# A two-layer hybrid backbone: the first stage in a fixed order, latent rows ahead of context rows

## The chip, the core and the metric

The kernel runs on one core of a Trainium2 chip. The metric is device time in microseconds of one execution. Three runs of the kernel before gave a median of 1833.99 us (1833.54 to 1836.31).

## What is computed

Layer 0 gives each row of `x` (256 latent tokens) and of `ctx` (256 context tokens), both 1024 wide, a modulated norm, and projects the result with one matrix. The part of the reference that the first stage computes:

```python
def modulate(x, g, shift, scale):
    return rms_norm(x, g) * (1 + scale) + shift

def ada_params(cvec, w, b):
    mod = jax.nn.silu(cvec) @ w + b
    return jnp.split(mod[..., None, :], 6, axis=-1)

# even_layer
mx = ada_params(c, ada_w, ada_b)          # for the latent rows
mc = ada_params(c_ctx, ada_w, ada_b)      # for the context rows
... = even_project(modulate(ctx, n1_g, mc[0], mc[1]), w_in, qn_g, kn_g)
... = even_project(modulate(x, n1_g, mx[0], mx[1]), w_in, qn_g, kn_g)
```

After it come retention and grouped attention over both streams, an out-projection and a dense SwiGLU (layer 0), then latent attention and top-2-of-8 SwiGLU experts (layer 1). The experts take more than half of the time and are not touched.

## The kernel before

All matmuls are in float32r, with the operand split in two: a rounded copy H (ScalarE, line 104) and the rest L (VectorE, line 105), so that one product takes three matmuls: H·H, L·H and H·L. Matmuls are in `mm` (line 85), transposes in `transpose` (line 213).

The first stage makes, for the 512 rows (token tiles t = 0, 1 latent, 2, 3 context; stream s = 0 latent, 1 context), the modulated input `X` and the product of it with columns 2048 to 2560 of `w_in` (called bq). The 1024 columns of `X` come in eight k tiles, in four parts q of two k tiles each:

- `norm_rows` (lines 303 to 322) takes the mean square of two row tiles on ScalarE (line 314), the reciprocal root by a dozen small VectorE operations (lines 185 to 197), and scales the rows (line 321 on VectorE, line 319 on ScalarE). `xn_T(s)` (line 453) transposes the rows on TensorE, and ScalarE copies them out of PSUM (line 459).
- `ada_loads(q)` (line 419) asks SP's queue for two 1 MB blocks of `l0_ada_w`. `ada_part(q)` (line 425) is 64 small matmuls with them (line 429), an add on VectorE (line 432), one transpose, and two VectorE operations for shift and scale (lines 437, 439).
- `bq_load(k)` (line 470) loads 256 KB of `w_in`. `bq_split(k)` splits it, applies scale and shift to both streams of one k tile (line 482, result `hf`), and splits that into `X`. `bq_mm(k)` (line 489) has 12 matmuls of 512 columns, over all four t.

The loop is at lines 496 to 512: in turn q it asks for the loads of q and the modulation loads of q+1, traces `ada_part(q)`, the matmuls of part q-1, and then the splits of part q. The order on an engine isn't this order: a scheduler with its own model of costs orders the instructions of each engine, by program order where several are ready in its model. `tc.keep_in_program_order(ins)` binds one instruction behind the one traced before it on its engine. Buffers with one tag are reused in turn, and the scheduler adds the waits for that.

The next unit of work, `rows_unit(X, w_in, 2560, ...)` at line 542 (called bkv: 96 matmuls of 256 columns), needs a 1 MB load, its split, and the two PSUM banks of tag mm, which ScalarE frees at line 526. Ahead of it on SP's queue stand, at lines 520 and 521, the rotary table and the broadcast of two 64-wide gains to 128 partitions and 8 and 2 heads; behind it the decay bands (line 543) and other small broadcasts (line 219). `Ada` (line 237) is the same modulation for later rows; it has its bias loads on ScalarE's queue (line 245). The decay masks of retention (`ret_masks`, line 729) take the tile `wb` from `bands`, in two ScalarE operations (lines 736 and 741).

Of the kernel before, what the change touches and what calls it, by code (L numbers as in the profile page):

```python
# [58 lines left out]
@with_exitstack  # L59
def hybrid_kernel(ctx: ExitStack, tc: tile.TileContext, i, out):  # L60
    nc = tc.nc
    ACT, DVE, PE = nc.scalar, nc.vector, nc.tensor


    const = ctx.enter_context(tc.tile_pool(name="const", bufs=1))
# [149 lines left out]
    def bcast_into(t, reps):  # L215

        c = 0
        for s, r, m in reps:
            nc.sync.dma_start(v3(t[:, c:c + r * m], r),
                              bass.AP(tensor=s.tensor, offset=s.offset, ap=[[0, P], [0, r], [1, m]]))  # L220
            c += r * m

# [134 lines left out]
    nc.gpsimd.memset(sil, 0.0)  # L357

    ACT.activation(sil[:, 0, 31:32], sil[:, 0, 30:31], AF.Silu)
    x_r = load_res("rx", i["x"])  # L360

    vec_list = [("c", 8), ("c_ctx", 8), ("l0_norm1_g", 8), ("l0_norm2_g", 8), ("l1_norm1_g", 8), ("l1_norm2_g", 8),
                ("l1_q_lora_g", 3), ("l1_kv_lora_g", 2)]
# [7 lines left out]
    def load_vecs(names):  # L371
        n = sum(dict(vec_list)[v] for v in names)
        vrow = modp.tile([P, 512], F32, tag="adarow", bufs=2, name=nm("vrow"))[:n, :P]
        r = 0
        for v in names:
            src = i[v]
            if len(src.shape) == 2:
                src = src.rearrange("o n -> (o n)")
            m = dict(vec_list)[v]
            (nc.scalar if len(names) > 2 else nc.sync).dma_start(vrow[r:r + m, :], src.rearrange("(a b) -> a b", b=P))  # L380
            r += m
        return vrow, vpos[names[0]], n

    def vecs_T(vrow, c0, n):
        ps = psum("T")
        transpose(ps[:, :n], vrow)
        DVE.tensor_copy(vecT[:, c0:c0 + n], ps[:, :n])

    vec_c = load_vecs(["c", "c_ctx"])
    c_r = load_res("rc", i["ctx"])  # L390

    vecs_T(*vec_c)
    for s, name in enumerate(("c", "c_ctx")):
# [6 lines left out]
    la = l0.enter_context(tc.tile_pool(name="la", bufs=1))  # L400
# [4 lines left out]
    def x_tiles(n):  # L405
        return [xp.tile([P, 4, 512], F32R, tag=tg, name="x1" + tg) for tg in X_TAGS[n]]
# [36 lines left out]
    sh1 = const.tile([P, KD, 2], F32, tag="sh1_0", name="sh1_0")  # L443
    xnT = [xp.tile([P, 4, 512], F32, tag=tg, name="xnT" + tg) for tg in ("a1", "a3")]
    loads = [ada_loads(0)]
    vec_g = load_vecs([n for n, _ in vec_list[2:]])
    for s in range(2):
        for a in range(2):
            nc.scalar.dma_start(adab[64 * a + s:64 * a + 64:32, :, :],
                              b_ada[1024 * a:1024 * a + 1024].rearrange("(q h c) -> h q c", h=2, c=P))  # L450
    xns = [norm_rows(x_r, la, "bv"), norm_rows(c_r, la, "bv", act=(1,))]

    def xn_T(s):
        for kp in range(KD // 2):
            ps = psum("S" if kp % 2 else "T")
            for kk in range(2):
                for t in range(2):
                    transpose(ps[:, kk * 256 + t * P:kk * 256 + (t + 1) * P], xns[s][t][:, tok(2 * kp + kk)])
            ACT.copy(xnT[kp // 2][:, 2 * (kp % 2):2 * (kp % 2) + 2, 256 * s:256 * s + 256], v3(ps[:, :], 2))

    xn_T(0)
    vecs_T(*vec_g)

    TOK = range(4)

# [4 lines left out]
    def bq_load(k):  # L470
        if k % 4 == 0:
            wbq["H", k // 4], wbq["L", k // 4] = ring_tile("H"), ring_tile("L")
        wbq[k] = lt.tile([P, 512], F32, tag="prob", bufs=4, name=nm("wbq"))
        nc.sync.dma_start(wbq[k], w_in[k * P:(k + 1) * P, 2048:2560])

    def bq_split(k):
        c = tok4(k)
        split_to(wbq["H", k // 4][:, c], wbq["L", k // 4][:, c], wbq[k])
        hf = lt.tile([P, 512], F32, tag="hf", bufs=2, name=nm("hf"))
        for s in range(2):  # L480
            cs = slice(256 * s, 256 * s + 256)
            DVE.tensor_scalar(hf[:, cs], xnT[k // 4][:, k % 4, cs], s1[:, k, s:s + 1], sh1[:, k, s:s + 1],
                              op0=ALU.mult, op1=ALU.add)
        split_to(X.H(k, slice(0, 512)), X.L(k, slice(0, 512)), hf)

    def tok4(k):
        return slice(512 * (k % 4), 512 * (k % 4) + 512)

    def bq_mm(k):
        H, L, c = wbq["H", k // 4], wbq["L", k // 4], tok4(k)  # L490
        for t in TOK:
            mm(ps_bq[t], X.H(k, tok(t)), H[:, c], k == 0, False)
            mm(ps_bq[t], X.L(k, tok(t)), H[:, c], False, False)
            mm(ps_bq[t], X.H(k, tok(t)), L[:, c], False, k == KD - 1)

    for q in range(5):
        if q < 4:
            for k in (2 * q, 2 * q + 1):
                bq_load(k)
            if q < 3:  # L500
                loads.append(ada_loads(q + 1))
            if q == 1:
                for l, t in zip((X.hs, X.ls), x_tiles(1)):
                    l.append(t)
            ada_part(q, loads[q])
        if q == 0:
            xn_T(1)
        for k in (2 * q - 2, 2 * q - 1) if q else ():
            bq_mm(k)
        if q < 4:  # L510
            for k in (2 * q, 2 * q + 1):
                bq_split(k)
# [4 lines left out]
    band = v3(cb[:, 0:1152], 3)  # L517
    ropeb = cb[:, 1152:1408].rearrange("p (t w c) -> p t w c", t=2, w=2)
    g10 = cb[:, 1408:2048]
    nc.sync.dma_start(ropeb, i["rope_b"])  # L520
    bcast_into(g10, [(i["l0_q_norm_g"], 8, 64), (i["l0_k_norm_g"], 2, 64)])

    qk = {}
    for t in TOK:
# [15 lines left out]
        DVE.reduce_sum(ss[:, 10 * t:10 * t + 10], v3(sq[:, :], 10), axis=AX.X)  # L540

    rows_unit(X, w_in, 2560, (2, 3, 0, 1), bkv_evac)
    nc.sync.dma_start(band, i["bands"])
    lgt = bcast_row(i["l0_ret_log_decay"].rearrange("a b -> (a b)"), 16, "lgt")
    lg256 = small.tile([P, 16], F32, tag="lg256", bufs=1, name="lg256")
    DVE.tensor_scalar(lg256, lgt, 256.0, None, op0=ALU.mult)
# [182 lines left out]
    def ret_masks(hp):  # L729

        W = []
        for hf in range(2):
            h = 2 * hp + hf
            wf = lt.tile([P, 2, 384], F32, tag="s3", bufs=4, name=nm("wf"))
            wb = lt.tile([P, 2, 384], F32, tag="wb", bufs=1, name=nm("wb"))
            ACT.activation(wb[:, 0, :], band[:, 2, :], AF.Identity, scale=lgt[:, 8 + h:9 + h])
# [1096 lines left out]
```

## Time and profile before

| | |
|---|---|
| median of three runs | 1833.99 us |
| the profiled execution | 1834.48 us |
| its span | 1832.7 us |
| TensorE busy | 1788.2 us, 98% of the span |
| VectorE, ScalarE, GpSimd busy | 1391.4, 1119.9, 14.2 us |
| from the start to the first bkv matmul | 58.10 us |

The time outside the span is 1.8 us. A row of the timeline has the start, the busy time of the merged instructions, engine, line, operation, output and inputs, and how many; in brackets stand the idle time ahead of it on its engine and what ended that. A row of the chain has start, duration and what it was. A row of the windows has busy time and instruction count of each engine, the granted clock of TensorE (1.00 is full speed), the busy share of the 16 DMA engines, and GB/s. A busy TensorE is not TensorE at its peak, since the ends of matmuls are modelled: rates are taken from starts.

### The profile page before, as it was taken

What the parts mean: (1) busy time and instruction counts of PE and PEld (TensorE: products, weight loads), DVE (VectorE), ACT (ScalarE), POOL (GpSimd) and SP (SyncE); (2) the same over time, 40 slices, a digit from 0 to 9 for tenths busy, and PEclk for the clock granted to TensorE, in tenths of its full rate; (3) what the DMA queues carried; (4) which work ended last, traced back from release to release, by engine and by line L of the source; (5) the groups of instructions that cost most, each with busy time, mean ns of one, the idle gap of its engine ahead of it and who ended that gap; (6) DMA issues with size and microseconds to landing.
All of it is one profiled execution on the core that took longest, in us unless ns stands there. A gap on an engine that the chain in (4) does not pass through costs nothing.

```text
span 1832.7 us, 23905 instructions
## 1 busy us (share of the span) xinstructions
PE 1788.2 (98%) x9410; PEld 1461.5 (80%) x9410; DVE 1391.4 (76%) x1739; ACT 1119.9 (61%) x1191; POOL 14.2 (1%) x24
## 2 busy tenths in 40 slices
PE   7899999999999999999999999999999999999997
PEld 5778668878779998677888888878878888788786
DVE  4688676424345668788889889898898898888887
ACT  4686543421223464567877777777767777777775
POOL 0000000000000000020000000000000000000000
PEclk9999999999999999999999999999999999999999
DMA  8443542343344566868998999999999999999992
GB/s 284 161 138 120 179 117 92 95 155 110 126 148 152 174 199 204 335 216 310 349 367 320 371 363 360 374 335 350 368 342 379 371 341 344 358 362 374 348 376 79
DMA packets 228730, 483.36 MB, mean 264 GB/s; under 512 B 11013, under 2 KB 65626, under 8 KB 223490
## 3 DMA queue, kind: packets, MB, share of 16 engines
q1 hardware_dynamic: 228416, 481.64, 73.7%
q8 instruction: 76, 1.25, 0.3%
q14 instruction: 44, 0.36, 0.1%
q10 hardware_dynamic: 194, 0.12, 0.0%
HBM read 480.68 MB, written 1.05 MB: 263 GB/s over the span
## 4 chain that ended last, share of the span: by engine, by line
PE 86%; DVE 6%; DMA 3%; ACT 2%; issue 1%; ACTq 0%; SPq 0%; DVEq 0%
PE ps L85 80%; PE ps L213 3%; DVE uL L105 3%; PE ps L258 2%; DMA uraw<-in_l_w_in_dram 1%; ACT uH L104 1%; DMA uraw<-in_l_exp_w_dram 0%; DMA uraw<-in_l_w_out_dram 0%; DMA raw<-in_l_exp_w_dram 0%; DVE rx L1705 0%; DMA rx<-in_x_dram 0%; PE ps L429 0%; DVE y L105 0%; DVE rst L194 0%; DMA xn<-in_l_exp_w_dram 0%
## 5 line engine op out<-in xcount | busy, mean ns | idle before, releaser
L85 PE MATMUL ps<-uH,xe 128*128 128x512 f32 x1792 | 450.8, 391 | 4.4 <-ACT uH L104 3.2
L85 PEld LDWEIGHTS ps<-uH,xe 128*128 128x128 f32 x1792 | 334.0, 188 | 76.2 <-ACT uH L104 5.3
L105 DVE TENSOR_TENSOR uL<-uraw,uH 128x2048 fp32r<-128x2048 f32 (+3 forms) x126 | 276.2, 2193 | 136.8 <-ACT uH L104 128.8
L104 ACT CAST uH<-uraw 128x2048 fp32r<-128x2048 f32 (+3 forms) x126 | 231.1, 1835 | 203.4 <-PE ps L85 163.5
L85 PE MATMUL ps<-uL,xe 128*128 128x512 f32 x896 | 244.4, 392 | 2.7 <-DVE uL L105 2.3
L105 DVE TENSOR_TENSOR uL<-h,uH 128x2048 fp32r<-128x2048 f32 x95 | 217.2, 2290 | 24.6 <-ACT uH L104 20.6
L85 PE MATMUL ps<-uH,aa 128*128 128x512 f32 x896 | 222.4, 390 | 0.0
L104 ACT CAST uH<-h 128x2048 fp32r<-128x2048 f32 x95 | 181.8, 1916 | 54.4 <-PE ps L85 47.9
L85 PEld LDWEIGHTS ps<-uL,xe 128*128 128x128 f32 x896 | 166.0, 188 | 41.9 <-DVE uL L105 8.6
L85 PEld LDWEIGHTS ps<-uH,aa 128*128 128x128 f32 x896 | 168.0, 188 | 35.2 <-issue 0.5
L85 PE MATMUL ps<-h,uH 128*128 128x256 f32 (+1 forms) x1008 | 176.7, 327 | 0.0
L85 PEld LDWEIGHTS ps<-h,uH 128*128 128x128 f32 x1008 | 150.8, 190 | 21.9 <-issue 3.2
L105 DVE TENSOR_TENSOR uL<-a,uH 128x2048 fp32r<-128x2048 f32 x60 | 137.4, 2290 | 16.8 <-ACT uH L104 14.6
L105 DVE TENSOR_TENSOR uL<-raw,uH 128x2048 fp32r<-128x2048 f32 (+1 forms) x60 | 135.2, 2254 | 15.2 <-ACT uH L104 14.2
L104 ACT CAST uH<-raw 128x2048 fp32r<-128x2048 f32 (+1 forms) x60 | 113.2, 1887 | 35.9 <-PE ps L85 35.4
L104 ACT CAST uH<-a 128x2048 fp32r<-128x2048 f32 x60 | 114.9, 1915 | 33.0 <-PE ps L85 32.9
L85 PE MATMUL ps<-uL,aa 128*128 128x512 f32 x448 | 123.4, 396 | 0.0
L85 PEld LDWEIGHTS ps<-uL,aa 128*128 128x128 f32 x448 | 81.4, 188 | 15.6 <-DVE uL L105 0.5
L85 PE MATMUL ps<-h,uL 128*128 128x256 f32 (+1 forms) x504 | 92.6, 326 | 0.0
L85 PE MATMUL ps<-uH,a 128*128 128x512 f32 x352 | 88.2, 391 | 1.1 <-ACT uH L104 1.1
L105 DVE TENSOR_TENSOR uL<-xp,uH 128x2048 fp32r<-128x2048 f32 (+1 forms) x34 | 76.9, 2262 | 10.3 <-ACT uH L104 9.9
L85 PEld LDWEIGHTS ps<-h,uL 128*128 128x128 f32 x504 | 76.9, 190 | 7.8
(384 smaller groups left out, 2364.4 us busy)
## 6 DMA issues: line engine op xcount, KB each, us to landing
h<-in_l_exp_w_dram SPq DMA_DIRECT2D x94, 1024.0 KB
uraw<-in_l_exp_w_dram SPq DMA_DIRECT2D x60, 1024.0 KB
a<-in_l_exp_w_dram SPq DMA_DIRECT2D x60, 1024.0 KB
raw<-in_l_exp_w_dram SPq DMA_DIRECT2D x58, 1024.0 KB
uraw<-in_l_ffn_w_dram SPq DMA_DIRECT2D x38, 1024.0 KB
uraw<-in_l_ada_w_dram SPq DMA_DIRECT2D x34, 1024.0 KB
xp<-in_l_exp_w_dram SPq DMA_DIRECT2D x30, 1024.0 KB
xn<-in_l_exp_w_dram SPq DMA_DIRECT2D x30, 1024.0 KB
```

What stands on the lines that cost most here:

```text
L85: PE.matmul(o, l, r, start=start, stop=stop)
L104: h = ACT.copy(H, src)
L105: l = DVE.tensor_sub(L, src, H.bitcast(F32))
L213: PE.transpose(o, in_, ident[:in_.shape[0], :in_.shape[0]])
L258: PE.matmul(self.ps[32 * j:32 * j + 32, :], sil[:, self.k, :], raw[:, 512 * j:512 * j + 512], start=(self.k == 0), stop=(self.k == KD - 1) ...
```

## The change

The diff, with repeated lines cut:

```diff
+    engines = nc.scalar, nc.vector, nc.tensor
+    ACT, DVE, PE = engines
+    class InOrder:
+        def __getattr__(self, name):
+            f = getattr(self.engine, name)
+            return lambda *a, **k: tc.keep_in_program_order(f(*a, **k))
 # bcast_into
-            nc.sync.dma_start(v3(t[:, c:c + r * m], r),
+            nc.gpsimd.dma_start(v3(t[:, c:c + r * m], r),
 # load_vecs
-            (nc.scalar if len(names) > 2 else nc.sync).dma_start(vrow[r:r + m, :], ...)
+            (nc.gpsimd if names[0] != "c" else nc.sync).dma_start(vrow[r:r + m, :], ...)
-    x_r = load_res("rx", i["x"])
     vec_c = load_vecs(["c", "c_ctx"])
-    c_r = load_res("rc", i["ctx"])
+    x_r = load_res("rx", i["x"])
     loads = [ada_loads(0)]
-    vec_g = load_vecs([n for n, _ in vec_list[2:]])
+    vec_g = load_vecs(["l0_norm1_g"])
-            nc.scalar.dma_start(adab[64 * a + s:64 * a + 64:32, :, :],
+            nc.gpsimd.dma_start(adab[64 * a + s:64 * a + 64:32, :, :],
-    xns = [norm_rows(x_r, la, "bv"), norm_rows(c_r, la, "bv", act=(1,))]
+    ACT, DVE, PE = (InOrder(e) for e in engines)
+    xns = [norm_rows(x_r, la, "bv")]
-    xn_T(0)
     vecs_T(*vec_g)
+    xn_T(0, (0, 1))
+    def bq_xsplit(q, s, between=None):
+        for kk in range(2):
+            DVE.tensor_scalar(hf[:, kk, :], xnT[g][:, r + kk, cs], s1[:, k, s:s + 1], sh1[:, k, s:s + 1], ...)
+        if between:
+            between()
+        split_to(X.hs[g][:, r:r + 2, cs], X.ls[g][:, r:r + 2, cs], hf)
+    def bq_mm(q, s):      # 12 matmuls: 4 H.H, then 4 H.L, then 4 L.H, of the two t of stream s
+    bq_loads(0)
+    c_r = load_res("rc", i["ctx"])
+    for q in range(4):
+        if q < 3:
+            bq_loads(q + 1)
+            loads.append(ada_loads(q + 1))
+        if q:
+            bq_wsplit(q)
+            bq_xsplit(q - 1, 1)
+            bq_mm(q - 1, 1)
+        ada_part(q, loads[q])
         if q == 0:
+            bq_xsplit(q, 0, lambda: bq_wsplit(0))
+        else:
+            bq_xsplit(q, 0)
+        bq_mm(q, 0)
+        if q == 0:
+            xn_T(0, (2, 3))
+            xns.append(norm_rows(c_r, la, "bv", act=(1,)))
+            xn_T(1)
+    bq_xsplit(3, 1)
+    bq_mm(3, 1)
+    ACT, DVE, PE = engines
+    vecs_T(*load_vecs([n for n, _ in vec_list[3:]]))
-    nc.sync.dma_start(ropeb, i["rope_b"])
-    bcast_into(g10, [(i["l0_q_norm_g"], 8, 64), (i["l0_k_norm_g"], 2, 64)])
+    nc.gpsimd.dma_start(ropeb, i["rope_b"])
+    for c, n, g in ((0, 8, "l0_q_norm_g"), (512, 2, "l0_k_norm_g")):
+        bcast_into(g10[:, c:], [(i[g], 1, 64)])
+        nc.gpsimd.tensor_copy(v3(g10[:, c + 64:c + 64 * n], n - 1), ...)
-    nc.sync.dma_start(band, i["bands"])
+    nc.gpsimd.dma_start(band, i["bands"])
 # ret_masks: both ScalarE operations that write wb (lines 736 and 741)
+            tc.keep_in_program_order(ACT.activation(wb[:, 0, :], ...))
+            tc.keep_in_program_order(ACT.activation(wb[:, 1, :], ...))
```

Between the two assignments of `ACT, DVE, PE` every instruction of these engines, those of helpers included, is bound behind the one traced before it on its engine. `bq_load` now takes both k tiles of a part in one 512 KB load, into four buffers of their own.

## Rows read from the trace of the kernel before

**Rows 1.** The page: busy time of the engines over the span.

```profile
PE 1788.2 (98%) x9410; PEld 1461.5 (80%) x9410; DVE 1391.4 (76%) x1739; ACT 1119.9 (61%) x1191; POOL 14.2 (1%) x24
```

**Rows 2.** Windows: PE, PEld, DVE, ACT, POOL busy (count), PEclk, DMA share, GB/s.

```profile
0.00:10.00 10.00, 0.26 (x1) 0.18 (x1) 1.12 (x8) 3.99 (x8) 1.65 (x11) 1.00 0.80 282
20.00:30.00 10.00, 8.67 (x99) 6.85 (x100) 5.46 (x16) 4.47 (x9) 0.00 (x0) 1.00 1.08 358
40.00:50.00 10.00, 8.83 (x91) 6.80 (x90) 4.27 (x12) 1.75 (x4) 0.53 (x1) 1.00 0.16 52
```

**Rows 3.** The chain that ended last, first 70 us: start, duration, what.

```profile
0.74 5.23 DMA rx<-in_x_dram
...
34.35 1.87 PE ps L429 x60
...
36.26 19.30 DMA uraw<-in_l_w_in_dram
```

**Rows 4.** Timeline of SP's queue, 30 to 50 us.

```profile
33.45 2.53 SPq L219 DMA_DIRECT2D cb<-in_l_k_norm_g_dram  x1
...
38.71 8.13 SPq L543 DMA_DIRECT2D cb<-in_bands_dram  x1
```

**Rows 5.** Timeline of TensorE where the first stage ends and bkv begins.

```profile
51.78 0.39 PE L85 MATMUL ps<-uL,x1h 128*128 128x512 f32 x1
...
54.50 0.39 PE L85 MATMUL ps<-uL,x1h 128*128 128x512 f32 x1
58.10 1.80 PE L85 MATMUL ps<-uH,x1a 128*128 128x256 f32 x8 [3.21 <-ACT qk L526]
...
62.57 1.12 PE L85 MATMUL ps<-uH,x1a 128*128 128x256 f32 x8
```

**Rows 6.** Window just behind that gap.

```profile
60.00:62.00 2.00, 2.00 (x12) 2.00 (x12) 0.05 (x1) 1.97 (x4) 0.00 (x0) 0.53 0.51 90
```

**Rows 7.** Timeline of the start: SP's queue, and the norm of the latent rows.

```profile
1.24 0.40 SPq L380 DMA_DIRECT2D vrow<-in_c_dram  x1
...
6.59 1.06 ACT L314 ACTIVATE xn<-rx 128x1024 f32<-128x1024 f32 x1 [4.35 <-DMA vrow<-in_l_q_lora_g_dram]
...
8.96 0.17 DVE L185 TENSOR_SCALAR rsa<-ms 128x2 f32<-128x2 f32 x1 [1.97 <-ACT xn L314]
...
11.02 1.42 DVE L321 TENSOR_SCALAR rx<-rx,rsy 128x1024 f32<-128x1024 f32 x2
```

**Rows 8.** Timeline: the last step of the context norm.

```profile
18.69 1.15 ACT L319 ACTIVATE rc<-rc,rsy 128x1024 f32<-128x1024 f32 x1 [1.47 <-DVE rsy L197]
```

**Rows 9.** Timeline: transposes of latent and context rows, and their copies out.

```profile
11.82 3.68 PE L213 MATMUL ps<-ident,rx 128*128 128x128 f32 x16 [5.05 <-DVE rx L321]
...
15.15 1.55 ACT L459 COPY xnTa<-ps 128x512 f32<-128x512 f32 x3
...
20.29 1.58 PE L213 MATMUL ps<-ident,rc 128*128 128x128 f32 x13
```

**Rows 10.** Timeline: from the end of part 1's matmuls to its split input.

```profile
28.03 0.29 DVE L432 TENSOR_TENSOR adarow<-ps,adab 128x128 f32<-128x128 f32 x1 [2.01 <-PE ps L429]
...
29.17 0.27 PE L213 MATMUL ps<-ident,adarow 128*128 128x128 f32 x1
...
29.75 1.38 DVE L482 TENSOR_SCALAR hf<-xnTa,s,sh 128x256 f32<-128x256 f32 x4
...
30.52 1.27 ACT L104 CAST x1a<-hf 128x512 fp32r<-128x512 f32 x2 [5.47 <-DVE hf L482]
```

**Rows 11.** Timeline: the split of two k tiles of the weights.

```profile
23.88 1.17 ACT L104 CAST uH<-wbq 128x512 fp32r<-128x512 f32 x2
...
24.74 1.29 DVE L105 TENSOR_TENSOR uL<-wbq,uH 128x512 fp32r<-128x512 f32 x2
```

**Rows 12.** Timeline of ScalarE: the table change for an early mask.

```profile
60.03 1.28 ACT L741 ACT_TABLE_LOAD   x1
```

**Rows 13.** Waits of TensorE, 54 to 260 us: total, times, longest.

```profile
PE ps L85 <- ACT qk L526: 3.2, 1, 3.2
PE ps L85 <- ACT osq L791: 1.3, 2, 0.8
```

More of the change, by code (lines that the diff above doesn't have):

```diff
@@ L61, in hybrid_kernel, with __init__ @@
     nc = tc.nc
-    ACT, DVE, PE = nc.scalar, nc.vector, nc.tensor
+    engines = nc.scalar, nc.vector, nc.tensor
+    ACT, DVE, PE = engines
+    class InOrder:
+        def __init__(self, engine):
+            self.engine = engine
+        def __getattr__(self, name):
+            f = getattr(self.engine, name)
+            return lambda *a, **k: tc.keep_in_program_order(f(*a, **k))
     const = ctx.enter_context(tc.tile_pool(name="const", bufs=1))
@@ L379, in load_vecs @@
             m = dict(vec_list)[v]
-            (nc.scalar if len(names) > 2 else nc.sync).dma_start(vrow[r:r + m, :], src.rearrange("(a b) -> a b", b=P))
+            (nc.gpsimd if names[0] != "c" else nc.sync).dma_start(vrow[r:r + m, :], src.rearrange("(a b) -> a b", b=P))
             r += m
@@ L445, in hybrid_kernel, with xn_T @@
     loads = [ada_loads(0)]
-    vec_g = load_vecs([n for n, _ in vec_list[2:]])
+    vec_g = load_vecs(["l0_norm1_g"])
     for s in range(2):
         for a in range(2):
-            nc.scalar.dma_start(adab[64 * a + s:64 * a + 64:32, :, :],
+            nc.gpsimd.dma_start(adab[64 * a + s:64 * a + 64:32, :, :],
                               b_ada[1024 * a:1024 * a + 1024].rearrange("(q h c) -> h q c", h=2, c=P))
-    xns = [norm_rows(x_r, la, "bv"), norm_rows(c_r, la, "bv", act=(1,))]
-    def xn_T(s):
-        for kp in range(KD // 2):
+    ACT, DVE, PE = (InOrder(e) for e in engines)
+    xns = [norm_rows(x_r, la, "bv")]
+    def xn_T(s, kps=range(KD // 2)):
+        for kp in kps:
             ps = psum("S" if kp % 2 else "T")
@@ L472, in bq_load @@
             wbq["H", k // 4], wbq["L", k // 4] = ring_tile("H"), ring_tile("L")
[L473 to L482, printed above, removed]
+        if k % 2 == 0:
+            w2 = lt.tile([P, 2, 512], F32, tag="pt", bufs=4, name=nm("wbq"))
+            nc.sync.dma_start(w2, w_src(w_in, k, 2, 2048, 512))
+            wbq[k], wbq[k + 1] = w2[:, 0, :], w2[:, 1, :]
@@ new lines, in bq_wsplit @@
+    def bq_wsplit(q):
+        for k in (2 * q, 2 * q + 1):
+            c = tok4(k)
+            split_to(wbq["H", k // 4][:, c], wbq["L", k // 4][:, c], wbq[k])
+    def bq_xsplit(q, s, between=None):
+        cs, g, r = slice(256 * s, 256 * s + 256), q // 2, 2 * (q % 2)
+        hf = lt.tile([P, 2, 256], F32, tag="hf", bufs=2, name=nm("hf"))
+        for kk in range(2):
+            k = 2 * q + kk
+            DVE.tensor_scalar(hf[:, kk, :], xnT[g][:, r + kk, cs], s1[:, k, s:s + 1], sh1[:, k, s:s + 1],
@@ L483, in bq_split @@
                               op0=ALU.mult, op1=ALU.add)
-        split_to(X.H(k, slice(0, 512)), X.L(k, slice(0, 512)), hf)
+        if between:
+            between()
+        split_to(X.hs[g][:, r:r + 2, cs], X.ls[g][:, r:r + 2, cs], hf)
     def tok4(k):
         return slice(512 * (k % 4), 512 * (k % 4) + 512)
[L489 to L494, printed above, removed]
@@ L496, in hybrid_kernel @@
-    for q in range(5):
-        if q < 4:
-            for k in (2 * q, 2 * q + 1):
[L499 to L505, printed above, removed]
-        if q == 0:
-            xn_T(1)
[L508 to L512, printed above, removed]
+    def bq_mm(q, s):
+        for k in (2 * q, 2 * q + 1):
+            H, L, c = wbq["H", k // 4], wbq["L", k // 4], tok4(k)
+            for t in (2 * s, 2 * s + 1):
+                mm(ps_bq[t], X.H(k, tok(t)), H[:, c], k == 0, False)
+        for k in (2 * q, 2 * q + 1):
+            H, L, c = wbq["H", k // 4], wbq["L", k // 4], tok4(k)
+            for t in (2 * s, 2 * s + 1):
+                mm(ps_bq[t], X.H(k, tok(t)), L[:, c], False, False)
+        for t in (2 * s, 2 * s + 1):
+            for k in (2 * q, 2 * q + 1):
+                mm(ps_bq[t], X.L(k, tok(t)), wbq["H", k // 4][:, tok4(k)], False, k == KD - 1)
@@ new lines, in bq_loads @@
+    def bq_loads(q):
+        for k in (2 * q, 2 * q + 1):
+            bq_load(k)
+    bq_loads(0)
[4 more added lines that the diff above has]
+            loads.append(ada_loads(q + 1))
+        if q == 1:
+            for l, t in zip((X.hs, X.ls), x_tiles(1)):
+                l.append(t)
+        if q:
[3 more added lines that the diff above has]
+        ada_part(q, loads[q])
+        if q == 0:
+            bq_xsplit(q, 0, lambda: bq_wsplit(0))
[5 more added lines that the diff above has]
+            xns.append(norm_rows(c_r, la, "bv", act=(1,)))
+            xn_T(1)
@@ L519, in hybrid_kernel @@
     g10 = cb[:, 1408:2048]
-    nc.sync.dma_start(ropeb, i["rope_b"])
-    bcast_into(g10, [(i["l0_q_norm_g"], 8, 64), (i["l0_k_norm_g"], 2, 64)])
+    nc.gpsimd.dma_start(ropeb, i["rope_b"])
+    for c, n, g in ((0, 8, "l0_q_norm_g"), (512, 2, "l0_k_norm_g")):
+        bcast_into(g10[:, c:], [(i[g], 1, 64)])
+        nc.gpsimd.tensor_copy(v3(g10[:, c + 64:c + 64 * n], n - 1), g10[:, c:c + 64].unsqueeze(1).to_broadcast([P, n - 1, 64]))
     qk = {}
@@ L735, in ret_masks @@
             wb = lt.tile([P, 2, 384], F32, tag="wb", bufs=1, name=nm("wb"))
-            ACT.activation(wb[:, 0, :], band[:, 2, :], AF.Identity, scale=lgt[:, 8 + h:9 + h])
+            tc.keep_in_program_order(ACT.activation(wb[:, 0, :], band[:, 2, :], AF.Identity, scale=lgt[:, 8 + h:9 + h]))
             DVE.scalar_tensor_tensor(wf[:, 0, :], band[:, 1, :], lgt[:, h:h + 1], wb[:, 0, :], op0=ALU.mult, op1=ALU.add)
@@ L740, in ret_masks @@
             ACT.activation(wf[:, 1, :], band[:, 0, :], AF.Exp, scale=lgt[:, h:h + 1], bias=lg256[:, h:h + 1])
-            ACT.activation(wb[:, 1, :], band[:, 0, :], AF.Exp, scale=nlg[:, h:h + 1], bias=lg256[:, 8 + h:9 + h])
+            tc.keep_in_program_order(
+                ACT.activation(wb[:, 1, :], band[:, 0, :], AF.Exp, scale=nlg[:, h:h + 1], bias=lg256[:, 8 + h:9 + h]))
             DVE.tensor_add(wf[:, 1, :], wf[:, 1, :], wb[:, 1, :])
```

## The prediction

> **What bounds the kernel now.** The page comes first: TensorE is busy for 98% of the span [rows 1], so time can only be won where it idles or runs slowly, and an edit of the first stage is worth what it does to the moment at which the next unit, bkv, starts. So I read next, by windows of 10 us, the first 60 us. Transfers fill the first 40 us: 282 GB/s in the first 10, and 358 at a full DMA share from 20 to 30 [rows 2]. From 40 to 50 the share is only 0.16, at 52 GB/s. The chain of waits says what that means: the 1 MB of bkv's weights, asked for at 36.26, land 19.30 us later and end the chain there [rows 3]. SP's queue shows why: the broadcast of the second gain takes 2.53 us to issue, the bands 8.13 us [rows 4]; what stands behind the broadcasts moves slowly. TensorE's timeline shows the price: bq's last matmul starts at 54.50, bkv's first at 58.10 after 3.21 us idle [rows 5], and the granted clock behind the gap is 0.53, its lower level of 1.2 GHz [rows 6]. The first 24 matmuls of bkv start from 58.10 to 62.57, 4.47 us; at the later rate (8 start in 0.95 to 1.12 us; I take 0.12 each [rows 5]) they would need 2.9. So the gap costs 3.2 + 1.6 us, and bkv is where it would be if it had started warm at 58.10 + 1.6 = 59.7. That is the number to beat.
>
> **The change part by part.** Loads first. Broadcasts, bands and rotary table go from SP to GpSimd, and the gains shrink to one copy each, with GpSimd doing the repeats. So bkv's 1 MB lands behind the last modulation weights: the hole of 3.2 + 1.6 us goes, whatever else happens. The moved loads queue on GpSimd behind the rotary table, which waits for the buffer of part 1's weights; their readers come after bkv, so I cost them at nothing. `x` goes behind two small loads on SP (0.40 us for the first; they are two [rows 7]), so it lands some 0.7 us after the 0.74 + 5.23 of now [rows 3], about 6.7; the squares start at 6.59 today, because ScalarE still issues vector loads, which are moved away. That is a draw.
>
> Now the fixed order. I lay the program order out on three engines, each strictly in order, with durations from rows:
>
> - Latent norm: squares from 6.6, 2.4 us to the first root operation (8.96), 2.06 us to the scaling (11.02), 1.42 for it [rows 7]: 12.5. Eight transposes at the 3.68/16 = 0.23 us of the cold start [rows 9]: 14.3.
> - Part 0: 64 small matmuls, 1.87 for 60, hence 2.0 warm [rows 3], some 2.7 while the clock rises: 17.0.
> - Then a wait that the fixed order lays open. Between a part's matmuls and the first bq matmul stand the add (0.29), the transpose (0.27), shift and scale (from 29.44 to 29.75), half of `hf` (29.75 to 30.52) and one cast (0.64) [rows 10]: 2.4 us with the hand-overs. Today bq matmuls of the part before lie in it; in the new order TensorE's next instruction is the one that waits. 19.4.
> - A block of 12 bq matmuls: from 51.78 to 54.50, 2.72 us for twelve starts [rows 5]. 22.1.
> - The rest of the latent transposes, eight at 1.58/13 = 0.12 [rows 9]: 23.1; ScalarE copies the last out at 0.52 each [rows 9]: 23.6.
> - Only now, on ScalarE, come the context squares, since they are traced behind those copies: 2.4 + 2.06 [rows 7] and 1.15 for the row tile that ScalarE scales [rows 8]: 29.3. Nothing else is next on TensorE: it idles from 23.1 to 29.3, 6.2 us. Before, this norm ran beside part 0.
> - Sixteen context transposes: 1.9 us warm, 3.7 cold [rows 9]. After an idle time of twice the 3.21 us that brought the lower clock I take cold: 33.0. Copies to 33.5, then (in ScalarE's order) two weight casts, 1.17, VectorE's subtraction behind them, 0.6 [rows 11], `hf` 0.8 and a cast 0.64 [rows 10]: first context matmul at 36.8. TensorE has idled another 3.8 us.
> - That block of 12 stands ahead of `ada_part(1)`. Cold, it loses what bkv's first 24 lost, 1.6, or, by the 0.53 over all its 2.72 us, 2.4; I take 2.0: it ends at 41.5. So part 1's matmuls start at 41.5; today their add is at 28.03 [rows 10], so they start near 26.
> - From here a part is 2.0 + 2.4 + 2.7 (latent) + 0.6 (the context cast is not yet done) + 2.7 (context) = 10.4 us: parts 1 and 2 end at 51.9 and 62.3. Part 3 takes 2.0 + 2.4 + 5.4: bq ends at 72.1. Weights are there long before.
> - bkv's cast and its two PSUM banks lie beside part 3 (the latent banks are done one block early), so bkv starts at about 72.1 with a warm clock.
>
> Against 59.7 this is +12.4 us. Bounds: no cold clock at 29 to 41 takes 1.8 + 2.0 off (+8.6). The other way, the scheduler may place bkv's own cast or subtraction between bound instructions; it has twice the columns of the 1.17 and 1.29 us in [rows 11], so it could hold up a split by some 2.5 (+14.9). I take 0, since both engines idle for most of a part.
>
> Last, the masks. The two `wb` operations of each head no longer run early: out of the hole goes a table change of 1.28 us [rows 12], and from the attention stage some mask work moves into retention. No row shows retention in that order. What it can give is bounded by TensorE's waits from 54 to 260 us: besides the hole, 2.8 us in five groups, 1.3 the largest [rows 13]. What it can cost is a wait of the same kind, which I bound by the same 2.8. I take 0, nearest to the small waits that are there.
>
> The sum: the profiled execution of 1834.5 us, 0.5 above the median, plus 12.4 is 1846.9; set against the median I say 1846.5. Its own range is 1834.0 + 8.6 - 2.8 = 1840 to 1834.0 + 14.9 + 2.8 = 1852.
>
> A rule of the Trainium skill speaks against the move to GpSimd. VectorE is busy for only 1.12 of the first 10 us [rows 2], in which the gain and bias loads must be issued. SBUF — State Buffer, section Who interferes with whom, says that some VectorE operations and GpSimd lock each other out of a shared pair of ports, and that GpSimd then can't write its DMA descriptors. By that rule the early loads have little to wait for here, and the trace of before has no DMA on GpSimd that would show it. As a mechanism of this kernel it is rival 3.
>
> **The rivals.**
> 1. *Data pace.* The order costs nothing, because context work is ready when wanted, and the stage ends with its last weights. The stream of 12.6 MB (in units of 2^20 bytes: 8 of modulation, 2 of bq, 2 of rows) at 0.358 MB per us from about 3 us [rows 2] lands by 39; then 2.0 + 2.4 + 5.4 give 48.8, against 59.7: -10.9, 1823. For it: TensorE's own work is only 8 blocks of 2.7, 4 times 2.0, 32 transposes (4 us) and some small ones, 35 us. Against it: the context squares stand behind the latent block on ScalarE by the program text. It decides from the point at which that norm is done before 23.
> 2. *The order stays much as it was* (the binding doesn't do what it says, or the scheduler fills the gaps): only the hole goes, -4.8, 1829. Against it: each instruction is bound to its predecessor, and of later work nearly everything needs the whole `X`.
> 3. *GpSimd is late.* The gain's transpose now stands ahead of the latent transposes on TensorE; if the load comes later than 12.5 us, everything shifts by the excess. VectorE's scaling, 1.42 us [rows 7], is the longest thing there that could hold it up twice: +3 on top, 1849.5.
> 4. *It cancels.* Warm clock, and masks worth their whole 2.8 us: 8.6 - 2.8 = +5.8; another 2 to 6 us would have to come from denser attention on the relieved ScalarE: 1834 to 1838.
>
> **How the numbers follow.** Forecast 0.67, rival 3 0.07, rival 4 0.08, rival 1 0.10, rival 2 0.08. About 0.2% (3.7 us) is what a measurement can tell from no change: slower 0.75, within 0.07, faster 0.18. The range goes down to rival 2's 1828, so that most of rival 1 and a little above 1853 stay out: 1828 to 1853. The forecast's own range is 1840 to 1852.
>
> **What would show it.** In the changed profile: no long landing of bkv's weights; TensorE idle for some 6 us at 23 and some 4 us ahead of the first context matmul, at a granted clock near 0.5; part 1's small matmuls starting near 41 and not 26; 2.4 us idle behind each part; parts 10.4 us apart; first bkv matmul at 70 to 74 with no gap ahead of it. I am wrong if the context squares run before 20 us, or if bkv starts before 60.

## The result: 21 us slower, and the profile after

The changed kernel takes 1854.99 us (1854.22 to 1855.22), the kernel before on the same chip 1833.76: a ratio of 1.0111 [1.0099, 1.0123]. The forecast was 1846.5 and its range ended at 1853. So the sign and the mechanism of the fixed order were right, and the size was too small: the profiled executions stand 20.6 us apart (1855.09 against 1834.48), not 12.4.

The page of the changed kernel, busy time of the engines over a span of 1853.2 us:

```profile
PE 1793.2 (97%) x9411; PEld 1464.5 (79%) x9411; DVE 1393.8 (75%) x1740; ACT 1123.2 (61%) x1191; POOL 25.8 (1%) x46
```

Against [rows 1] TensorE has gained 5 us of busy time with one matmul more, and some 15 us of idle time. Of the 20.5 us between the spans 19.7 are there when bkv starts (77.79 against 58.10 us). TensorE's timeline up to it, without the small matmuls of parts 1 to 3 (L73 is now the line of every bound instruction):

```profile
11.94 0.47 PE L73 MATMUL ps<-ident,rx 128*128 128x128 f32 x1 [4.54 <-DVE rx L73]
...
15.36 2.59 PE L73 MATMUL ps<-uraw,sil 128*32 128x128 f32 x60 [0.43 <-DMA uraw<-in_l_ada_w_dram]
18.41 0.33 PE L73 MATMUL ps<-ident,adarow 128*128 128x128 f32 x1 [0.45 <-DVE adarow L73]
20.56 2.08 PE L73 MATMUL ps<-uH,x1a 128*128 128x512 f32 x4 [1.82 <-ACT x1a L73]
...
24.82 1.03 PE L73 MATMUL ps<-ident,rx 128*128 128x128 f32 x8
31.69 3.98 PE L73 MATMUL ps<-ident,rc 128*128 128x128 f32 x16 [5.84 <-issue]
39.49 2.08 PE L73 MATMUL ps<-uH,x1a 128*128 128x512 f32 x4 [3.82 <-ACT x1a L73]
...
49.02 1.19 PE L73 MATMUL ps<-uH,x1a 128*128 128x512 f32 x4 [1.75 <-ACT x1a L73]
...
59.64 1.19 PE L73 MATMUL ps<-uH,x1h 128*128 128x512 f32 x4 [1.74 <-ACT x1h L73]
...
70.28 1.22 PE L73 MATMUL ps<-uH,x1h 128*128 128x512 f32 x4 [1.75 <-ACT x1h L73]
71.33 1.88 PE L73 MATMUL ps<-uL,x1h 128*128 128x512 f32 x4
73.01 2.84 PE L73 MATMUL ps<-uH,x1h 128*128 128x512 f32 x8
...
77.79 1.21 PE L96 MATMUL ps<-uH,x1a 128*128 128x256 f32 x8
```

The last line is bkv: it starts warm at 77.79, with no gap ahead of it (3.21 us in [rows 5]), where the number to beat was 59.7. The two large holes (5.84 and 3.82 us) and the three waits of 1.75 us are the fixed order. Four lines of windows show the clock in the slow blocks (same columns as [rows 2]):

```profile
20.00:24.00 4.00, 3.44 (x9) 2.78 (x10) 1.65 (x3) 0.50 (x1) 0.00 (x0) 0.57 1.09 351
31.00:35.00 4.00, 3.24 (x14) 2.97 (x15) 0.59 (x1) 2.47 (x4) 0.00 (x0) 0.50 1.08 360
39.00:45.00 6.00, 5.51 (x28) 4.17 (x32) 0.69 (x1) 0.44 (x1) 0.00 (x0) 0.58 0.01 2
70.00:75.00 5.00, 4.71 (x14) 3.71 (x15) 2.03 (x4) 1.49 (x4) 0.00 (x0) 0.66 0.92 314
```

Two of the four, 31 to 35 and 39 to 45, stood in the prediction. The others, 20 to 24 and 70 to 75, did not.

ScalarE's timeline shows why TensorE stood still at 26 to 32: the context squares come only behind the last copy of the latent rows.

```profile
25.45 1.07 ACT L73 COPY xnTa<-ps 128x512 f32<-128x512 f32 x2 [4.95 <-PE ps L73]
26.41 1.07 ACT L73 ACTIVATE xn<-rc 128x1024 f32<-128x1024 f32 x1
...
31.01 1.15 ACT L73 ACTIVATE rc<-rc,rsy 128x1024 f32<-128x1024 f32 x1 [2.26 <-DVE rsy L73]
```

Past the first stage the distance grows once more, while attention runs. Retention begins with eight matmuls on `rqk`. The first of them is the 900th matmul behind bkv's first in both kernels, counted in the traces, with the same matmuls in another order between. Before and after:

```profile
188.79 1.13 PE L85 MATMUL ps<-rqk,rqk 64*128 64x256 f32 x8
```

```profile
208.82 1.13 PE L96 MATMUL ps<-rqk,rqk 64*128 64x256 f32 x8
```

That is 130.69 us behind bkv's start before, of which 1.6 are its slow start (the prediction's number), and 131.03 after: +1.9 us. From there to the first matmul of layer 1 that reads the tile `o`, 3390 matmuls later, both take the same time (604.95 and 604.64).

### The profile page after: what moved, and what is told of

The parts are those of the page before. It is cut to its first block, busy times and chain, and to the rows that moved or that the text cites. A ratio compares the mean times of both kernels' runs of the same rounds, so it can differ in the third digit from the quotient of the medians.

```text
span 1853.2 us, 23903 instructions
## 1 busy us (share of the span) xinstructions
PE 1793.2 (97%) x9411; PEld 1464.5 (79%) x9411; DVE 1393.8 (75%) x1740; ACT 1123.2 (61%) x1191; POOL 25.8 (1%) x46
## 4 chain that ended last, share of the span: by engine, by line
PE 86%; DVE 7%; ACT 3%; DMA 2%; issue 1%; SPq 0%; DVEq 0%; ACTq 0%
PE ps L96 79%; PE ps L224 3%; DVE uL L116 2%; PE ps L269 2%; PE ps L73 2%; ACT uH L115 1%; DMA uraw<-in_l_ada_w_dram 1%; DMA uraw<-in_l_w_in_dram 1%; DMA raw<-in_l_exp_w_dram 0%; DVE rx L1747 0%; DVE y L116 0%; DVE hf L73 0%; DMA uraw<-in_l_exp_w_dram 0%; DVE smx L359 0%; DVE uL L73 0%
```

## The experiments

### 1. Is it the binding?

The kernel after, without the line that binds the first stage:

```diff
-    ACT, DVE, PE = (InOrder(e) for e in engines)
```

> The changed kernel, with the binding of the first stage taken out and nothing else: loads, loop and masks stay as changed, and the scheduler orders the instructions again. If the fixed order is the cause (theory O), the idle time between 25.9 and 31.7 us and the one ahead of 39.49 go, bkv starts near 55 with no gap, and the time comes to 1828 to 1836 us, level with or below the kernel before. If the moved loads are the cause (rival L), bkv starts late here too, at 70 or later, and the time stays above 1848.

1842.31 us (1840.88 to 1843.74), ratio 1.005 [1.0033, 1.0066]; bkv at 64.97. This lies between the two ranges. 12.7 us of the 21 come with the binding. But a free scheduler does not get back to the time before either: with the new program order and load order, and with the masks still bound, the kernel stays some 8 us slower. Which of these it is was not tried without the binding. With it, the order was changed piece by piece (experiments 3, 5 and 6); the loads and masks were changed in both kernels (2, 4, 7, 9 and 10).

### 2. Are the moved loads worth their hole?

The kernel before, with only its broadcasts, rotary table and bands on GpSimd:

```diff
 # bcast_into
-            nc.sync.dma_start(v3(t[:, c:c + r * m], r),
+            nc.gpsimd.dma_start(v3(t[:, c:c + r * m], r),
-    nc.sync.dma_start(ropeb, i["rope_b"])
-    bcast_into(g10, ...)
-    nc.sync.dma_start(band, i["bands"])
+    nc.gpsimd.dma_start(ropeb, i["rope_b"])
+    for c, n, g in ((0, 8, "l0_q_norm_g"), (512, 2, "l0_k_norm_g")):
+        bcast_into(g10[:, c:], [(i[g], 1, 64)])
+        nc.gpsimd.tensor_copy(...)
+    nc.gpsimd.dma_start(band, i["bands"])
```

> The kernel before, with the broadcasts, the rotary table and the bands alone moved to GpSimd's queue (gains as one copy, repeated by GpSimd). Theory O: only the hole ahead of bkv goes, 3.2 us and 1.6 of slow clock, so 1828 to 1831 us, with bkv starting at about 55. Rival L: GpSimd's loads hold something up, and the time is 1834 or more.

1835.49 us, ratio 1.0007 [0.9997, 1.0017]: nothing gained, although the hole of [rows 5] is gone (bkv starts warm). ScalarE's timeline shows a new one:

```profile
40.12 0.62 ACT L738 ACTIVATE wb<-cb,lgt 128x384 f32<-128x384 f32 x1 [5.02 <-DMA cb<-in_bands_dram]
40.74 1.28 ACT L743 ACT_TABLE_LOAD   x1
42.04 0.71 ACT L743 ACTIVATE wb<-cb,lg,nlg 128x384 f32<-128x384 f32 x1
42.65 1.12 ACT L104 CAST uH<-wbq 128x512 fp32r<-128x512 f32 x2
```

An early mask is next on ScalarE and waits 5.02 us for the bands. Behind it stands the cast of the weights of bq's part 2, and TensorE waits 2.7 us for what follows; bkv starts at 61.11. The start is late as well: part 0's 60 small matmuls begin at 19.27, in the kernel before at 16.25 (experiments 7 and 9).

### 3. Context norm earlier

```diff
         bq_xsplit(q, 0)
+        if q == 0:
+            xns.append(norm_rows(c_r, la, "bv", act=(1,)))
         bq_mm(q, 0)
         if q == 0:
             xn_T(0, (2, 3))
-            xns.append(norm_rows(c_r, la, "bv", act=(1,)))
             xn_T(1)
```

> The changed kernel, with the context norm traced one place earlier: between the latent split of part 0 and its matmuls, so that ScalarE squares the context rows while TensorE has the latent block. Everything is still bound. Theory O: the idle time of 5.84 us shrinks below 1 and the context transposes run warm (1.9 instead of 4.0), so part 1 starts 7 to 10 us earlier and the time is 1845 to 1848. Rival L or a rival that blames the masks alone: less than 2 us change, 1853 to 1856.

1846.82 us, ratio 1.0071 [1.0054, 1.0088], as expected of the fixed order; bkv at 70.59, 7.2 us earlier. TensorE's timeline: no gap between latent and context transposes, and these at full pace.

```profile
26.09 1.03 PE L73 MATMUL ps<-ident,rx 128*128 128x128 f32 x8
26.96 2.19 PE L73 MATMUL ps<-ident,rc 128*128 128x128 f32 x16
33.34 2.07 PE L73 MATMUL ps<-uH,x1a 128*128 128x512 f32 x4 [4.20 <-ACT x1a L73]
```

### 4. What do the bound masks cost?

The kernel after, with both `wb` operations free:

```diff
-            tc.keep_in_program_order(ACT.activation(wb[:, 0, :], ...))
+            ACT.activation(wb[:, 0, :], ...)
-            tc.keep_in_program_order(
-                ACT.activation(wb[:, 1, :], ...))
+            ACT.activation(wb[:, 1, :], ...)
```

> The changed kernel with the two mask operations of each head unbound, as before. Between bkv and the experts the changed kernel loses another 2 us or so. If the masks' new place is the cause (rival M), the time falls by 1.5 to 2.5 us to 1852.5 to 1853.5; if that is only the scheduler's other choices, it stays within 1 us of 1855.

1855.45 us (1851.7 to 1857.41), ratio 1.0112 [1.0095, 1.0129]: the same time. By that alone the masks would be acquitted. The trace says otherwise. Here retention starts at

```profile
208.90 1.13 PE L96 MATMUL ps<-rqk,rqk 64*128 64x256 f32 x8
```

and bkv at 79.28, so the way between takes 129.62 us, 1.4 less than in the kernel after. Over all kernels of this study it is 130.8 to 131.6 wherever the masks are bound and 128.3 to 129.6 wherever they are free (the kernel before counted without its slow start). From there to layer 1's first matmul on `o` the two groups don't differ (603.8 to 605.5, 604.3 to 605.3). So the bound masks cost 1.4 to 2 us, in attention and not in retention. TensorE's idle time on the way is 2.4 us in both kernels, so this isn't a wait of TensorE; what it is instead isn't shown. In this execution the gain was lost at two other places: bkv started 1.5 us later (part 0's 60 matmuls took 3.32 us for 2.59), and one wait for `o` in layer 1, 1.2 us after the change, was 2.7.

The expectations of experiments 10 and 11 go by another measure, the distance of the first two blocks of eight tiny matmuls on `osq`: 20.02 us in the kernel before (217.04 to 237.06) and 21.72 after (235.22 to 256.94). It is no measure of time lost. Before:

```profile
215.15 1.13 PE L85 MATMUL ps<-rqk,rqk 64*128 64x256 f32 x8
217.04 1.02 PE L85 MATMUL ps<-ones,osq 128*128 128x2 f32 x8 [0.76 <-ACT osq L791]
...
237.06 1.05 PE L85 MATMUL ps<-ones,osq 128*128 128x2 f32 x8 [0.57 <-ACT osq L791]
```

After:

```profile
235.22 1.02 PE L96 MATMUL ps<-ones,osq 128*128 128x2 f32 x8 [0.45 <-ACT osq L833]
236.10 0.71 PE L96 MATMUL ps<-x1h,uH 128*128 128x512 f32 x2
236.74 1.13 PE L96 MATMUL ps<-rqk,rqk 64*128 64x256 f32 x8
...
256.94 1.05 PE L96 MATMUL ps<-ones,osq 128*128 128x2 f32 x8 [0.53 <-ACT osq L833]
```

With bound masks the first block stands ahead of ten matmuls that precede it with free masks, and the distance is longer by these ten (236.10 to 237.80, 1.7 us). It comes out at 21.7 to 22.2 wherever the masks are bound and at 20.0 to 20.1 wherever they are free, and that its difference is close to the masks' price is chance.

### 5 and 6. The modulation part ahead of the context block

```diff
-        if q:
-            bq_wsplit(q)
-            bq_xsplit(q - 1, 1)
-            bq_mm(q - 1, 1)
-        ada_part(q, loads[q])
+        if q:
+            bq_wsplit(q)
+            bq_xsplit(q - 1, 1)
+        ada_part(q, loads[q])
+        if q:
+            bq_mm(q - 1, 1)
```

> The kernel after, with one pair of calls in the loop swapped: the modulation part of turn q is traced ahead of the context matmuls of part q-1, so that these twelve matmuls lie in the wait between the part's small matmuls and its first latent matmul. Theory (the fixed order costs what the program text puts in a row): the 1.75 us of idle time ahead of the first latent matmul of parts 1, 2 and 3, and the 0.6 ahead of the context block, go; a part takes 8.3 to 9 us instead of 10.6, bkv starts 5 to 7 us earlier, at 71 to 73, and the time is 1848 to 1850. Rival (the parts are paced by something else, the loads or ScalarE's and VectorE's splits): parts stay at 10 to 10.6 us and the time is 1853 to 1855.

1845.33 us (1843.02 to 1849.53), ratio 1.0062 [1.0044, 1.0081]; bkv at 69.28, 8.5 us earlier, more than expected. The gain is also in part 1: its small matmuls run from 36.34 in what was the second hole.

With the edit of experiment 3 as well:

> The kernel after with two changes of program order: the context norm ahead of the first latent matmuls, and each modulation part ahead of the context matmuls of the part before. Theory: the two gains add, 8.2 us of the one run alone and 5 to 7 of the other, bkv starts at 63 to 65 and the time is 1839.5 to 1842. If it is still slower than the kernel before by 5 us or more, late first loads and the low clock are what is left. Rival: both remove the same idle time, then it is no better than the better of the two, 1846 to 1848.

1839.7 us (1837.34 to 1841.69), ratio 1.0027 [1.0018, 1.0036]; bkv at 62.66. The two gains, 7.2 and 8.5, make 15.1 together: they add. The order of the program text is worth some 15 of the 20 us.

### 7. Loads and bound masks without the rest

Experiment 2, with the two `keep_in_program_order` of `ret_masks` from the change.

> The kernel before with two parts of the change alone: broadcasts, rotary table and bands on GpSimd, and the two operations that write wb bound in program order. With the loads alone the hole ahead of bkv went, but ScalarE took up an early mask, waited for the bands for 5.0 us and changed its table, and the time stayed at 1835.5. Theory (that early mask is what gave the gain back): no mask before retention, bkv starts warm at 57 to 59 and the time is 1828.5 to 1831.5. Rival (masks done early are worth about as much as they cost, since retention has to make them later): 1833 to 1836.

1832.69 us (1830.54 to 1834.84), ratio 0.999 [0.9981, 0.9999], between the two expected ranges. The mask was to blame for the hold-up of experiment 2: bkv starts at 57.02. But the bound masks cost 2.1 us in attention (from bkv's first matmul to retention 131.49 us, 129.43 in experiment 2), and the first 20 us are slower than before, which led to experiment 9: part 0's 60 matmuls start at 19.20, where the kernel before has them at 16.25.

### 8. How much is the clock?

The kernel after, with transposes of the identity put into TensorE's waits; no result depends on them:

```diff
+    def fill(n, tag):
+        ps = psum(tag)
+        for _ in range(n):
+            transpose(ps[:, :P], ident)
...
         bq_xsplit(q, 0)
+        if q in (0, 3):
+            fill(14, ("o", "ada")[q // 3])
         bq_mm(q, 0)
         if q == 0:
             xn_T(0, (2, 3))
+            fill(46, "o")
             xns.append(norm_rows(c_r, la, "bv", act=(1,)))
             xn_T(1)
+            fill(30, "o")
```

> The kernel after with transposes of the identity, whose results nothing reads, in four of TensorE's waits: 14 ahead of the first latent block, 46 ahead of the context transposes, 30 ahead of the first context block, 14 ahead of the last latent block; each about 0.12 us and a little fewer than the wait holds. Theory C (the low clock behind the waits costs some 7 us on top of the waits): the first latent block falls from 4.26 to 2.7 us, the context transposes from 4.0 to 2, the first context block from 5.06 to 2.8, the last 24 from 7.34 to 5.5; bkv starts at 70 to 72 and the time is 1846.5 to 1849. Rival (the low clock has another cause, or these blocks wait for something that the clock hides): the blocks keep their length and the time is 1853 to 1857.

1850.14 us (1848.7 to 1851.93), ratio 1.0084 [1.0069, 1.01]; bkv at 72.62. All four blocks behind a filled wait run at full pace. TensorE's timeline has, in turn, the first latent block, the context transposes, the first context block, part 1's latent block (its wait was not filled) and the last 24 matmuls.

```profile
20.91 1.20 PE L73 MATMUL ps<-uH,x1a 128*128 128x512 f32 x4 [0.29 <-ACT x1a L73]
...
22.85 1.07 PE L73 MATMUL ps<-uH,x1a 128*128 128x512 f32 x4
...
31.17 1.86 PE L73 MATMUL ps<-ident,rc 128*128 128x128 f32 x15 [0.24 <-ACT rc L73]
...
36.99 1.19 PE L73 MATMUL ps<-uH,x1a 128*128 128x512 f32 x4 [0.69 <-ACT x1a L73]
...
44.41 1.33 PE L73 MATMUL ps<-uH,x1a 128*128 128x512 f32 x4 [1.75 <-ACT x1a L73]
45.53 1.91 PE L73 MATMUL ps<-uL,x1a 128*128 128x512 f32 x4
...
66.79 1.20 PE L73 MATMUL ps<-uH,x1h 128*128 128x512 f32 x4 [0.22 <-ACT x1h L73]
```

That is 5.2 us at bkv of the 7 expected, and the time is a little above the expected range. Part of the rest was lost at another place: behind the wait that was not filled, ahead of part 1's latent block (44.41), the clock now falls. In the kernel after, the same wait of 1.75 us ahead of 49 left it at 1.00. The windows of experiment 8 and of the kernel after:

```profile
46.00:50.00 4.00, 4.00 (x13) 3.18 (x12) 1.62 (x4) 0.62 (x1) 0.75 (x2) 0.66 0.81 230
```

```profile
49.00:53.00 4.00, 3.76 (x15) 2.83 (x16) 3.24 (x6) 1.64 (x3) 0.00 (x0) 1.00 1.04 304
```

### 9. Why do the first weights land late?

Experiment 7 with the broadcasts for later stages (decay, four gains of layer 1, iota) back on SP:

```diff
-    def bcast_into(t, reps):
+    def bcast_into(t, reps, queue=nc.gpsimd):
...
 # bcast_row
-        bcast_into(t, [(src, 1, n)])
+        bcast_into(t, [(src, 1, n)], nc.sync)
```

and the same for iota.

> The kernel before with the rotary table, the two gains and the bands on GpSimd and the wb operations bound, as in the run with loads and masks, but the seven broadcasts of later stages (decay, four gains, iota, asked for by GpSimd at 1.9 to 5.6 us there) back on SP. Theory D (these small-packet transfers, done at 7 to 11 us, take the engines from the stream, which moves 90 GB/s at 9 to 10 us against 374 before, and make part 0's weights land late): the stream stays above 300 GB/s from 6 to 15, the 60 small matmuls of part 0 start near 16.3 instead of 19.2, bkv starts at 54 to 55 instead of 57.0, and the time is 1829.5 to 1831. Rival (the dip comes from the order of the large loads, or part 0's delay is taken up later anyway): bkv at 56.5 to 57.5 and 1832 to 1833.5.

1830.39 us (1828.87 to 1833.25), ratio 0.9977 [0.9968, 0.9986]; the 60 matmuls start at 16.26 and bkv at 53.47, 3.6 us earlier. The broadcasts are in the change too. GpSimd's timeline of the kernel after:

```profile
2.63 2.23 POOL L459 DMA_DIRECT2D adab<-in_l_ada_b_dram  x4
4.85 0.59 POOL L230 DMA_DIRECT2D lgt<-in_l_ret_log_decay_dram  x1
...
9.69 0.54 POOL L230 DMA_DIRECT2D iota<-in_iota_dram  x1
46.80 0.54 POOL L559 DMA_DIRECT2D cb<-in_rope_b_dram  x1 [36.57 <-PE ps L73]
```

The scheduler has put six loads (168 KB in all by the view of DMA issues; the expectation says seven) that the first stage doesn't need at the start of a queue that was free. One-microsecond windows of the kernel after show what the stream of weights pays:

```profile
8.00:9.00 1.00, 0.00 (x0) 0.00 (x0) 0.00 (x0) 1.00 (x2) 0.00 (x0) 1.00 1.13 293
9.00:10.00 1.00, 0.00 (x0) 0.00 (x0) 0.83 (x6) 0.04 (x1) 0.84 (x2) 1.00 1.26 65
10.00:11.00 1.00, 0.00 (x0) 0.00 (x0) 1.00 (x10) 0.00 (x0) 0.23 (x1) 1.00 0.88 253
```

The engines are full (1.26) at 65 GB/s; in the kernel before, the same microsecond has a share of 1.08 at 374 GB/s. Back on SP, in the kernel after:

```diff
-        bcast_into(t, [(src, 1, n)])
+        bcast_into(t, [(src, 1, n)], nc.sync)
```

> The kernel after with the broadcasts of later stages (decay, four gains, iota) back on SP; gains, bias, rotary table and bands stay on GpSimd. Theory D: no dip to 65 GB/s at 9 to 10 us, part 0's small matmuls follow the transposes without a wait and bq's first weights land by 17, so bkv starts 1 to 1.5 us earlier (76.3 to 76.8) and the time is 1853 to 1854. Rival: bkv unchanged at 77.5 to 78 and the time 1854.5 to 1855.5.

1853.47 us (1852.72 to 1855.06), ratio 1.0106 [1.009, 1.0121]; bkv at 77.01. The window from 9 to 10:

```profile
9.00:10.00 1.00, 0.00 (x0) 0.00 (x0) 0.78 (x6) 0.09 (x1) 0.00 (x0) 1.00 1.09 334
```

The dip is gone, and the 64 small matmuls follow the transposes without a wait; 0.8 us at bkv, a little less than expected. By the times alone the two kernels could not be told apart: the intervals overlap. In the fixed order part 0's weights are asked for at 1.99, ahead of the small loads, and less is lost than in experiment 7 (3.6), where they are asked for at 6.30, behind them.

### 10. The part of the change that pays

The kernel before with the rotary table and the two gains on GpSimd alone. Bands and later broadcasts stay on SP, the masks free:

```diff
-    nc.sync.dma_start(ropeb, i["rope_b"])
+    nc.gpsimd.dma_start(ropeb, i["rope_b"])
-    bcast_into(g10, [(i["l0_q_norm_g"], 8, 64), (i["l0_k_norm_g"], 2, 64)])
+    for c, n, g in ((0, 8, "l0_q_norm_g"), (512, 2, "l0_k_norm_g")):
+        bcast_into(g10[:, c:], [(i[g], 1, 64)], nc.gpsimd)
+        nc.gpsimd.tensor_copy(...)
```

> The kernel before with the rotary table and the two gains on GpSimd alone: bands and the broadcasts of later stages stay on SP, the wb operations stay free. Theory M (bound masks cost 1.7 us between the first and the second osq of retention, 21.72 instead of 20.02; free masks cost only where ScalarE takes one up before its bands are there): 20.0 between these two, and if ScalarE isn't held by the bands, bkv starts at 53.5 to 56 and the time is 1827.5 to 1830. Rival (ScalarE takes the early mask ahead of a cast again): TensorE waits 2 to 6 us at 45 to 55, bkv starts at 58 to 62 and the time is 1832 to 1836.

1827.95 us (1826.9 to 1828.62), ratio 0.9962 [0.9948, 0.9975]: faster than both kernels, by 5.8 us against the one before. bkv starts at 52.92, and retention 128.94 us behind it, as elsewhere with free masks:

```profile
52.92 1.12 PE L85 MATMUL ps<-uH,x1a 128*128 128x256 f32 x8
```

ScalarE still takes an early mask and its table change, but now behind bkv's own cast, where nobody waits:

```profile
47.84 1.91 ACT L104 CAST uH<-uraw 128x2048 fp32r<-128x2048 f32 x1
49.65 0.61 ACT L738 ACTIVATE wb<-cb,lgt 128x384 f32<-128x384 f32 x1
50.28 1.28 ACT L743 ACT_TABLE_LOAD   x1
```

### 11. The fixed order, mended

The kernel after with the edits of experiments 3, 4, 5 and 9 together, and the bands back on SP.

> The kernel after with its fixed order kept and the measured causes mended together: context norm ahead of the first latent matmuls, each modulation part ahead of the context matmuls of the part before, broadcasts of later stages and bands back on SP, wb operations free. Theory (the causes add): from 62.66 of the run with both changes of order, 0.8 to 1.3 less for the first loads, so bkv at 61 to 62; 20.0 between the first two osq; hence some 2.5 to 3 us below the 1839.7 of that run, 1836 to 1838, still above the kernel before, since the first latent blocks keep a low clock. Rival (one of them falls away in company, such as ScalarE taking an early mask into the stage): 1839 to 1842.

1833.45 us (1832.75 to 1835.64), ratio 0.9997 [0.9988, 1.0006]; bkv at 60.36. It lies below the expected range by 2.5: the parts gain more together than I added up, and the bands' way back had no run of its own. The 21 us are gone, with the binding still in place. But this kernel has the moved loads that make experiment 10 faster, and it stands 5.5 us behind that one, where the scheduler orders. So the fixed order, as mended here, still costs; whether another fixed order would not, no run shows.

## Why the prediction was right and wrong

Right, step by step. The latent transposes end at 14.36 (14.3 forecast). The wait of part 0, from the end of its matmuls to the first bq matmul, is 2.6 us (2.4). TensorE idles 5.84 ahead of the context transposes (6.2), which take 3.98 (3.7, cold). It idles 3.82 ahead of the first context matmul (3.8). From the end of the first latent block to that matmul the sum had 14.7 us, and the trace has 24.82 to 39.49, 14.67; so close it is by luck, since two of the errors cancel. A part takes 10.65 and 10.62 (10.4). bkv follows without a gap. Experiments 3, 5 and 6 confirm the cause: the two places in the program text named by the prediction hold 15 us. Of the transposes, [rows 9] have the cold 3.68 and the warm 1.58 for 13; after the change the context rows take 3.98, and in experiment 3, without the idle time ahead, 2.19.

What failed is the price of the first stage, 5.7 us too small at bkv, and the 0 for the masks. Too small were five terms. Together they are 7.6 of the 8.1 us between +12.4 and +20.5 (by the spans); of the rest, the wait for `o` in layer 1 has 0.4 (1.24 us for 0.82).

- *First weights.* The first bq matmul was put at 19.4 and starts at 20.56: +1.2. The step that failed is the sentence that the moved loads queue on GpSimd behind the rotary table. That holds for the loads of lines 520, 521 and 543 (46.80 to 48.43), but `bcast_into` serves the later broadcasts too, and those went to the front. The second run of experiment 9, with them back on SP, gives back 0.85 of the 1.2: the first bq matmul starts at 19.71. The rest is mostly the wait behind part 0. I had costed the move at nothing without going through all callers of the changed line.
- *First latent block.* Forecast warm at 2.72, measured 4.26 at a granted clock of 0.57: +1.5. Here the step that failed is the choice of where the low clock comes: I had asked about the clock only where TensorE would idle for more than 3.21 us [rows 5]; here the waits were 0.43, 0.45 and 1.82.
- *Parts and the context block.* 5.06 for 4.7, and twice 0.23 us: +0.8.
- *Last part.* 11.97 us (65.82 to 77.79) for 9.8: +2.2. The low clock from 71 to 75 is again behind a wait of 1.75 us. Experiment 8 fills it and the 24 matmuls take 5.7 instead of 7.3 us. The sum had them warm, at 5.4: the same step.
- *Masks.* Taken at 0 with bounds of 2.8 either way; up to retention they cost 1.9 us against the kernel before, 1.4 against experiment 4. The step that failed is the price taken from TensorE's small waits [rows 13]: the prediction looked for the cost as such a wait, in retention. It lies in attention, at an idle time of TensorE that is the same with masks bound and free (2.4 us).

So of the 8.1 us some 3.5 are clock, 0.9 loads and 1.4 to 1.9 masks; the rest are small terms. The prediction knew that the low clock could come and priced it in two blocks, and it came in four. Its range contained a cold stage only where the idle time was long.

On the rivals: 1 (data pace) and 2 (order stays) fell with bkv at 77.79. Rival 3, GpSimd late with the gain, did not occur: the load is issued at 1.94 and takes 5.2 us to land by the view of DMA issues, thus lands at 7.1, ahead of the latent scaling at 11. The rule behind it (the Trainium skill, SBUF — State Buffer, section Who interferes with whom) had little to act on: the issues take 0.54 to 0.70 us each, and VectorE was busy for 1.00 of the first 10 us; these runs neither confirm it nor speak against it. GpSimd's loads did harm in another way, by filling the DMA engines from 9 to 10 us. Rival 4 needed denser attention; it took 1.9 us longer.

The number to beat holds within 2 us. Without the hole bkv was to start at 54.9 (59.7 less 4.8); experiments 9 and 10 have it at 53.47 and 52.92.

## What to carry to other kernels

Before an engine's order is bound by hand, lay the program text out as a queue for each engine: what stands behind a wait there is what the scheduler had been moving for you, and two lines of program order were worth 15 us here. When a helper's queue is changed, go through all its callers: a load that becomes free to start starts at once, and takes the DMA engines from the load that the first matmul needs. Take from a change the part that removes the measured hole: alone it was 5.8 us faster than the kernel before. And a distance between two marks on an engine compares two kernels only where the same work lies between them.

## What the runs showed that I had not expected

- The granted clock fell to its lower level (0.50, 1.2 GHz) not only behind idle times of 5.8 and 3.8 us, but in the first latent block, behind waits of 0.43, 0.45 and 1.82 us, and from 71 to 75, behind one of 1.75 us, after which TensorE was busy without a break. Two waits of the same length, at 49 and 60, did not bring it down, and when experiment 8 filled four waits, the fall moved to one that had been harmless. Which of several short waits is paid for at the low clock could not be told from their length here. That filling a wait with work holds the clock up in the block behind it is shown for all four places.
- Small broadcasts can fill the DMA engines at 65 GB/s (share 1.26), where large loads move 374 in the same microsecond of the kernel before. Six of them, 168 KB, cost part 0 three microseconds in experiment 7 (its 60 matmuls start at 19.20, and at 16.26 with the six on SP).
- One wait for `o` in layer 1, far from every edit, was 1.2 us after the change, 1.6 in experiment 10 and 2.7 to 2.8 in experiments 4 and 9. In these three the granted clock has a mean of 0.96 over 40 us around it instead of 1.00; the same wait of 1.6 in experiments 3 and 11 left it at 1.00. From the first matmul on `o` to the end the kernel after takes 1039.7 us, experiments 4 and 9 take 1042.4 and 1041.3. The cause stays open.
